# A feed forward in one unit of 1024 tokens, with Strassen's product in both projections

## The chip, the cores and the metric

The kernel runs on one NeuronCore of a Trainium2 chip. The metric is the device time of one execution in microseconds (us). Five engines take part: TensorE (PE, matmuls; PEld is its weight load), VectorE (DVE), ScalarE (ACT), GpSimd (POOL), and SyncE (SP), which here only issues DMA transfers.

## The reference

One layer of a streaming encoder for a prompt of 1024 tokens and 128 sample tokens (8 sequences of 16). The change is in its last step, the feed forward:

```python
D_MODEL = 1024
D_FF = -(-8 * D_MODEL // (3 * 256)) * 256        # 2816

def swiglu(x, w_in, w_out):
    g, u = jnp.split(x @ w_in, 2, axis=-1)
    return (jax.nn.silu(g) * u) @ w_out

def post_blocks(x, mix, mk, mv, w_mem_q, w_mem_o, w_ffn_in, w_ffn_out, ln_g, ln_b):
    x = layer_norm(ALPHA * x + mix, ln_g[0], ln_b[0])
    x = layer_norm(ALPHA * x + mem_attention(x, mk, mv, w_mem_q, w_mem_o), ln_g[1], ln_b[1])
    x = layer_norm(ALPHA * x + swiglu(x, w_ffn_in, w_ffn_out), ln_g[2], ln_b[2])
    return x
```

All data are float32. What comes ahead (the combined input projection, a gated linear recurrence, sliding window attention, the output projection, attention into 256 memory tokens) computes the same before and after.

## The kernel before, in words

*Precision.* A float32 operand is split into a part that a fast matmul keeps (`hi`, type fp32r; a ScalarE cast, L132) and a rest (`lo`, a VectorE subtraction, L133). A product is three matmuls: hi by hi, lo by hi, hi by lo (`mm3`, L93).

*Tokens.* Nine tiles of 128 rows; the third is the sample's. They go through the layer in three groups of three tiles. `mem_kv` projects the memory tokens and stores them from `kv_sb` to DRAM; then phase 2 starts, whose first matmuls belong to `out_proj` (weights `w_out`). The last step ahead of the feed forward is `mem_out` of group 2. The rows after the second norm are in DRAM (`x2_dram`; the profile names it x_scratch).

*Feed forward.* Two units: tiles 0 to 3 (512 tokens) and tiles 4 to 8 (640). `unit_operands` transposes a unit's rows (L97) and makes the seven right operands B11, T1, T2, B22, T3, B21, T4 of Winograd's form of Strassen's product, each in hi and lo; POOL makes the differences (L933). Tokens are halved, so a product has 256 or 320 columns. `hidden` computes two tiles of the hidden features, 11 pairs for a unit: four weight tiles of 128x1024 (512 KB) are loaded from `in_w_f`, their sums are made on POOL (L970, L975) and DVE (L974, L979), each of seven products has 24 matmuls, and ACT and DVE add the products up and apply the gate (`th`, L995 to L1001). The hidden features stay on the chip. `ffn` goes over parts of the features: some pairs of `hidden`, then `proj_rows`, the second projection, as a plain product with 512 columns that is added to the rows by DVE (L705). The second unit's operands are made while the first unit's last part runs.

*Order.* The code is a set of generators with ranks (`Order`): the one of the lowest rank whose operands should be ready goes on, on a clock that counts the cost of matmuls alone. A scheduler behind it then sets each engine's own order. Loads, and stores too, all go through SP's one queue, in order; one that waits holds up those behind it. Weights are loaded into three buffers (`w_raw`).

Of the kernel before, what the change touches and what calls it, by code (L numbers as in the profile page):

```python
# [18 lines left out]
P = 128  # L19
# [16 lines left out]
# tokens go in the order of ORDER: two tiles of the prompt, the samples (tile 8), the other tiles of the prompt  # L36
# [6 lines left out]
class Event:  # L43
    """a point on TensorE's clock from which a result is expected to be there"""
# [34 lines left out]
class TensorE:  # L79
    """TensorE with the products' cost added to the clock of an Order"""  # L80
# [19 lines left out]
def trunk(ctx, tc, I, O):  # L100
# [10 lines left out]
    wp = pool("wp")  # L111
# [6 lines left out]
    def bank(name):  # L118
        return pp[name][0].tile([P, 512], F32, name=name, bufs=pp[name][1])
# [41 lines left out]
    class Quads(list):  # L161
        """feature-major blocks [P, GW] in two parts, four to a slot"""
# [40 lines left out]
    def fm(wsrc, x, which="a", n=GW, w=None):  # L203
        """one block of columns, feature major"""
# [9 lines left out]
    ident = const.tile([P, P], F32, name="ident")  # L214
    make_identity(nc, ident)
    tri = const.tile([P, 640], U8, name="tri")
    own = const.tile([P, 8], F32, name="own")
    sinks = const.tile([P, 8], F32, name="sinks")
    sinks_s = const.tile([P, 2], F32, name="sinks_s")
    gnorm = const.tile([P, P], F32, name="gnorm")  # L220
# [3 lines left out]
    carry = const.tile([P, HGH, P], F32, name="carry")  # L224
    V.memset(carry, 0.0)
    starts = [const.tile([P, GW], F32, name=f"starts{i}") for i in range(2)]
# [142 lines left out]
    def hgrn(g, h, xt, tm):  # L369
# [53 lines left out]
        def body():  # L423
# [14 lines left out]
            # from chunks to pairs of chunks  # L438
# [45 lines left out]
    def hgrn_sample(h, qg, kdt, v, at, pl, po, sv):  # L484
        """the sample's tile: a chunk and a state for each of its sequences"""
# [25 lines left out]
    def finish(sb, mx, sk, nk):  # L511
        """rows of sb [P, n, .]: exp(s - max), normalised with the sink's share"""
# [12 lines left out]
    def swa_tile(p1, ip, t, pos, q, ak, av):  # L525
        """heads 2 ip and 2 ip + 1 of both groups, one tile of queries over its own and the preceding tile of keys"""
# [105 lines left out]
    def proj_rows(src, wsrc, evac, which, ahead=(), nt=GT, by_tile=False):  # L632
        """rows of nt tiles; src: blocks [P, nt * P] in two parts"""
# [205 lines left out]
    def mem_sample(p2, qf, ot, ready):  # L839
# [5 lines left out]
        def cache():  # L845
            """the next part of the caches, four sequences to a tile"""
# [55 lines left out]
    class Unit:  # L902
        def __init__(self, t0, nt, pieces, tmp, row, th):
            self.t0, self.nt, self.n = t0, nt, nt * 64
            self.pieces, self.tmp, self.row, self.th = pieces, tmp, row, th
            self.ready = Event()

        def operand(self, op, kt):
            for k0, hi, lo in self.pieces[op]:
                if k0 <= kt < k0 + hi.shape[1]:  # L910
                    return hi[:, kt - k0], lo[:, kt - k0]

    def unit_operands(u):
        """a unit's rows, transposed, to the products' operands in two parts"""
        rows = [u.row() for _ in range(u.nt)]
        for t in range(u.nt):
            for q, r in enumerate(rows[t]):
                nc.sync.dma_start(out=r, in_=x2_dram[u.t0 + t][:, q * 512:(q + 1) * 512])
        yield 4000.0
        for t in range(u.nt):  # L920
            b = {}
            for q in range(2):
                ps = transposes(rows[t][q])
                st = u.tmp("stage")
                S.copy(st[:, :512], ps)
                v = st[:, :512].rearrange("p (k e c) -> p k e c", k=4, e=2)
                for e in range(2):
                    b[f"B{q + 1}{e + 1}"] = v[:, :, e]
            tt = [u.tmp("tt")[:, :512].rearrange("p (a k c) -> p a k c", a=2, k=4) for _ in range(2)]
            for n in range(4):  # L930
                b[f"T{n + 1}"] = tt[n // 2][:, n % 2]
            for o, x, y in (("T1", "B12", "B11"), ("T3", "B22", "B12"), ("T2", "B22", "T1"), ("T4", "B21", "T2")):
                G.tensor_tensor(b[o], b[x], b[y], op=ALU.subtract)  # L933
            c = slice(t * 64, t * 64 + 64)
            for o in OPS:
                for k0, hi, lo in u.pieces[o]:
                    src = b[o][:, k0:k0 + hi.shape[1]]
                    S.copy(hi[:, :, c], src)
                    (G if o == "T4" else V).tensor_tensor(lo[:, :, c], src, hi[:, :, c].bitcast(F32), op=ALU.subtract)  # L939
# [320 lines left out]
```

## Time and profile before

| | us |
|---|---|
| median of 3 runs | 1669.98 (1669.64 to 1675.53) |
| profiled execution | 1669.8 (its span) |
| PE busy | 1618.8 (97%) |
| DVE busy | 1235.5 (74%) |
| ACT busy | 735.8 (44%) |
| POOL busy | 244.2 (15%) |
| feed forward's first matmul | 858.45 |

The profile is of one execution, and its span is the whole of that execution's time as far as it is recorded. A row of a group gives line, engine, operation, output and inputs, shape and count, then busy us, mean ns of one, the idle time ahead and what ended it. Matmul records overlap: each one's own length (280 to 390 ns) is longer than the distance between two starts, and it is the distance that counts.

### The profile page before, as it was taken

The page shows a single profiled execution, that of the slowest core. Times are in us where ns is not written, and L with a number is a line of the kernel's source. Part 1 is how long each engine was busy: PE and PEld are TensorE (multiplying, and loading weights), DVE is VectorE, ACT ScalarE, POOL GpSimd, SP SyncE. Part 2 cuts the span into 40 slices and gives each one's busy share as a digit, 9 for nine tenths or more (in the row PEclk, how much of TensorE's full clock was granted, in tenths as well). Part 3 has the DMA queues.
Part 4 walks back from the last instruction along what each step waited for, and adds up shares of the span by engine and source line. Part 5 has one row for each costly group of instructions (what it writes and reads, how often), then busy time and mean ns, then how long its engine had stood idle before and what let it go on. Part 6 is the DMA issues. An engine that isn't in the chain of part 4 may idle for free. (4 is left out here: it accounts for less than half of the span.)

```text
span 1669.8 us, 26720 instructions
## 1 busy us (share of the span) xinstructions
PE 1618.8 (97%) x10341; PEld 1477.3 (88%) x10341; DVE 1235.5 (74%) x2161; ACT 735.8 (44%) x1471; POOL 244.2 (15%) x234
## 2 busy tenths in 40 slices
PE   8999999999999999999988999999989999999998
PEld 7998999999878987879878898989888999989896
DVE  6887688788568666787799577667898757566568
ACT  4543455445543555224645244345543424334241
POOL 1111121111000000000232110212232111111111
PEclk9999999999999999999999999999999999999999
DMA  7453343333884588646332523132543313131231
GB/s 244 128 179 125 93 151 102 105 115 108 277 313 149 169 274 311 234 138 227 101 114 91 176 89 127 64 101 91 175 168 122 101 58 107 51 101 64 89 100 65
DMA packets 84800, 233.65 MB, mean 140 GB/s; under 512 B 10048, under 2 KB 28352, under 8 KB 84672
## 3 DMA queue, kind: packets, MB, share of 16 engines
q1 hardware_dynamic: 84672, 231.93, 42.4%
q8 instruction: 81, 1.33, 0.3%
q14 instruction: 47, 0.39, 0.1%
HBM read 210.86 MB, written 20.97 MB: 139 GB/s over the span
## 5 line engine op out<-in xcount | busy, mean ns | idle before, releaser
L133 DVE TENSOR_TENSOR w_lo<-w_raw,w_hi 128x1024 fp32r<-128x1024 f32 (+1 forms) x279 | 343.1, 1232 | 166.4 <-ACT w_hi L132 165.5
L132 ACT CAST w_hi<-w_raw 128x1024 fp32r<-128x1024 f32 (+1 forms) x279 | 290.0, 1041 | 323.8 <-PE a L93 147.0
L93 PE MATMUL a<-w_hi,h 128*128 128x512 f32 x756 | 242.6, 394 | 5.2 <-DVE rows L705 2.6
L93 PE MATMUL a<-w_hi,q_hi 128*128 128x256 f32 (+1 forms) x576 | 197.0, 344 | 3.5 <-ACT w_hi L132 2.9
L93 PE MATMUL a<-w_lo,q_hi 128*128 128x256 f32 (+1 forms) x576 | 197.0, 342 | 1.9 <-DVE w_lo L133 1.8
L93 PE MATMUL a<-w_hi,q_lo 128*128 128x256 f32 (+1 forms) x576 | 195.4, 339 | 0.0
L93 PE MATMUL a<-q_hi,w_hi 128*128 128x384 f32 x528 | 186.8, 354 | 6.8 <-ACT q_hi L132 4.3
L93 PE MATMUL a<-q_hi,w_lo 128*128 128x384 f32 x528 | 180.1, 341 | 0.0
L93 PE MATMUL a<-q_lo,w_hi 128*128 128x384 f32 x528 | 179.9, 341 | 0.0
L93 PEld LDWEIGHTS a<-w_hi,h 128*128 128x128 f32 x756 | 141.8, 188 | 38.5 <-ACT h L1000 3.6
L132 ACT CAST w_hi<-w_s 128x1024 fp32r<-128x1024 f32 x88 | 92.2, 1048 | 181.3 <-PE a L93 87.9
L133 DVE TENSOR_TENSOR w_lo<-w_s,w_hi 128x1024 fp32r<-128x1024 f32 x88 | 134.6, 1533 | 35.9 <-ACT w_hi L132 35.9
L93 PE MATMUL a<-w_lo,h 128*128 128x512 f32 x378 | 148.2, 392 | 0.0
L970 POOL TENSOR_TENSOR w_s<-w_raw 128x1024 f32<-128x1024 f32 x22 | 54.8, 2492 | 490.6 <-DMA w_raw<-in_w_f_dram 428.7
L93 PE MATMUL a<-x,w_hi 128*128 128x256 f32 x704 | 126.3, 280 | 0.0
L93 PEld LDWEIGHTS a<-w_hi,q_hi 128*128 128x128 f32 x576 | 108.5, 188 | 17.9 <-ACT w_hi L132 3.3
L705 DVE SCALAR_TENSOR_TENSOR rows<-rows,a 128x512 f32<-128x512 f32 x123 | 82.7, 682 | 55.6 <-PE a L93 55.4
L93 PEld LDWEIGHTS a<-w_lo,q_hi 128*128 128x128 f32 x576 | 108.6, 189 | 16.8 <-DVE w_lo L133 3.4
L93 PEld LDWEIGHTS a<-w_hi,q_lo 128*128 128x128 f32 x576 | 108.6, 188 | 12.7 <-issue 0.5
L93 PEld LDWEIGHTS a<-q_hi,w_hi 128*128 128x128 f32 x528 | 100.6, 191 | 11.7 <-ACT q_hi L132 4.4
L93 PEld LDWEIGHTS a<-x,w_hi 128*128 128x128 f32 x704 | 108.1, 188 | 0.3
L93 PEld LDWEIGHTS a<-q_lo,w_hi 128*128 128x128 f32 x528 | 100.8, 191 | 1.9 <-issue 0.9
(247 smaller groups left out, 3662.5 us busy)
## 6 DMA issues: line engine op xcount, KB each, us to landing
w_raw<-in_w_f_dram SPq DMA_DIRECT2D x110, 512.0 KB, 3.6
w_raw<-in_w_fm_dram SPq DMA_DIRECT2D x41, 512.0 KB, 4.1
w_raw<-in_w_tm_dram SPq DMA_DIRECT2D x24, 512.0 KB, 3.6
w_raw<-in_w_out_dram SPq DMA_DIRECT2D x24, 512.0 KB, 5.4
w_raw<-in_w_mq_dram SPq DMA_DIRECT2D x24, 512.0 KB, 4.4
w_raw<-in_w_mo_dram SPq DMA_DIRECT2D x24, 512.0 KB, 4.1
w_s<-in_w_f_dram SPq DMA_DIRECT2D x22, 512.0 KB, 4.4
ln_gb<-in_ln_dram SPq DMA_DIRECT2D x16, 512.0 KB, 6.7
```

The costliest lines, as they stand in the source:

```text
L93: return self.eng.matmul(out, lhsT, rhs, **kw)
L132: S.copy(hi, src)
L133: V.tensor_tensor(lo, src, hi.bitcast(F32), op=ALU.subtract)
L705: V.scalar_tensor_tensor(y[t][:, hs], y[t][:, hs], scale, ps, op0=ALU.mult, op1=ALU.add)
L970: G.tensor_tensor(s1, a21, a22, op=ALU.add)
```

## The change

The prompt's eight tiles become one unit: 1024 tokens, 512 columns a product. `all_operands` makes its operands after `mem_out` of group 2. The first projection runs for all 11 pairs (`hidden`), with all sums of weights on POOL, and ends with the hidden features' own Strassen operands, of which seven a pair are stored to DRAM (`h_scratch`, L1051). The second projection then follows as a second stage: weights from two tiles a pair with sums on POOL (`prepare`), the operands of the features loaded again (`hq`, L1132), five parts of the pairs, two sets of blocks of 256 tokens. The sample's tile no longer belongs to a unit: its hidden features come by plain float32 matmuls of 128 columns (`sample_hidden`, run by `filler` at rank 10), in part beside `all_operands`, the rest during the second projection; they too go through DRAM (`hs_scratch`). Pools are closed and opened between the stages, the buffers of one stage lying where those of another were. The last norm puts half of its scaling on ACT and POOL (`final_norm`). The diff's core:

```diff
-UNITS = ((0, 4, ((0, 6), (6, 12), (12, 16), (16, 22))),
-         (4, 5, ((0, 2), (2, 6), (6, 10), (10, 14), (14, 18), (18, 22))))
+TILES = (0, 1, 3, 4, 5, 6, 7, 8)
+SAMPLE = 2
+PAIRS = FT // 2
+PARTS = ((0, 3), (3, 5), (5, 7), (7, 9), (9, 11))
...
+    def sample_hidden(i):
+        ps = bank("b")
+        for e in range(2):
+            w = []
+            for q in range(2):
+                w.append(ff["sample_w"]())
+                nc.sync.dma_start(out=w[q], in_=I["w_f1"][i, e * 2 + q])
+            for z in range(2):
+                for kt in range(KT):
+                    T.matmul(ps[:, cols(e * 2 + z)], w[kt // 4][:, cols(z * 4 + kt % 4)], xs[:, kt],
+                             start=kt == 0, stop=kt == KT - 1)
...
+        nc.sync.dma_start(out=hs_dram[:, i], in_=h)
...
     def hidden(f1, ops, i):
...
+            t = f1.tile([P, 1024], F32, name=name, tag="w", bufs=8)
...
+        G.tensor_tensor(s1, a21, a22, op=ALU.add)
+        G.tensor_tensor(s2, s1, a11, op=ALU.subtract)
+        G.tensor_tensor(a21, a11, a21, op=ALU.subtract)
+        G.tensor_tensor(s4, a12, s2, op=ALU.subtract)
...
+        gated(th[1], [(a, X[0], X[1]), (b, m1[0], m1[1])])
+        G.tensor_tensor(t2, th[1][:, b], t1, op=ALU.subtract)
+        G.tensor_tensor(th[0][:, b], th[1][:, b], th[0][:, b], op=ALU.subtract)
+        G.tensor_tensor(t4, th[1][:, a], t2, op=ALU.subtract)
+        for o, src in (("T2", t2), ("B22", th[1][:, b]), ("T3", th[0][:, b]), ("B21", th[1][:, a]), ("T4", t4)):
+            store(o, src)
...
+        def f2w(name):
+            return f2.tile([P, 1024], F32, name=name, tag="w", bufs=5)
+
+        def prepare(i):
+            w0, w1, s12, s34 = (f2w(x) for x in ("w0", "w1", "s12", "s34"))
+            for n, t in enumerate((w0, w1)):
+                nc.sync.dma_start(out=t, in_=I["w_f2"][n, i])
...
+            G.tensor_tensor(s1, a21, a22, op=ALU.add)
+            G.tensor_tensor(s2, s1, a11, op=ALU.subtract)
+            G.tensor_tensor(s4, a12, s2, op=ALU.subtract)
+            G.tensor_tensor(s3, a11, a21, op=ALU.subtract)
...
+                S.copy(hi, src)
+                (G if name in ("A21", "A22") else V).tensor_tensor(lo, src, hi.bitcast(F32), op=ALU.subtract)
...
+            nc.sync.dma_start(out=q, in_=h_dram[bs[0] // 2, OPS.index(o), :, i0:i1, c:c + n])
+            S.copy(hi, q)
+            (G if o in ("T1", "T3", "T4") else V).tensor_tensor(lo, q, hi.bitcast(F32), op=ALU.subtract)
...
+        for i in range(PARTS[0][1]):
+            prepare(i)
+        for b in range(4):
+            for e in range(2):
+                y[b, e] = f2.tile([P, 1024], F32, name="y", bufs=8)
+                out_rows(x2_dram, b, e, y[b, e], None)
...
+            yield from blocks(part, (0, 1), last)
+            yield from filled(part[1])
+            yield from sample(part, n == 0, last)
...
+            yield from blocks(part, (2, 3), last)
+            for _ in range(*part):
+                if len(prepared) < PAIRS:
+                    prepare(len(prepared))
```

How the instructions stand at the places that the prediction speaks of. First SP's queue where phase 2 begins, before (kv_sb is what `mem_kv` stores):

```order
L143 DMA w_raw<-in_w_out_dram 128x1024
L199 DMA raw<-mix_scratch 128x384 x2
L264 DMA out_dram<-kv_sb 128x512
L266 DMA mem_kv_scratch<-kv_sb 128x256 x2
L264 DMA out_dram<-kv_sb 128x512
L266 DMA mem_kv_scratch<-kv_sb 128x256 x2
L143 DMA w_raw<-in_w_out_dram 128x1024
L714 DMA rows<-in_xtok_dram 128x1024 x3
L143 DMA w_raw<-in_w_out_dram 128x1024
L264 DMA out_dram<-kv_sb 128x512
```

And the same place after:

```order
L719 DMA rows<-in_xtok_dram 128x1024 x3
L689 DMA ln_gb<-in_ln_dram 128x1024 x2
L269 DMA out_dram<-kv_sb 128x512
L271 DMA mem_kv_scratch<-kv_sb 128x256 x2
L269 DMA out_dram<-kv_sb 128x512
L271 DMA mem_kv_scratch<-kv_sb 128x256 x2
L148 DMA w_raw<-in_w_out_dram 128x1024 x3
L204 DMA raw<-mix_scratch 128x384 x2
```

The first three loads of w_out stood ahead of the last stores of kv_sb; now they stand behind them.

TensorE after the last `mem_out`, before (x, B and T are a unit's operands):

```order
L93 MATMUL a<-w_lo,q_hi 128x512
L93 MATMUL a<-w_hi,q_lo 128x512
L93 MATMUL a<-x_9109,w_hi 128x256
L93 MATMUL a<-x_9110,w_hi 128x256
L93 MATMUL a<-x_9109,w_lo 128x256
```

And after (xs is the sample's transposed rows, x_row a tile's rows):

```order
L95 MATMUL a<-w_lo,q_hi 128x512
L95 MATMUL a<-w_hi,q_lo 128x512
L95 MATMUL b<-xs,w_raw 128x128 x20
L99 MATMUL b<-ident,x_row 128x128 x8
L95 MATMUL b<-xs,w_raw 128x128 x16
L99 MATMUL b<-ident,x_row 128x128 x8
L95 MATMUL b<-xs,w_raw 128x128 x16
```

A unit's products followed directly; now the operands' transposes and the sample's matmuls stand between.

SP's queue where the first projection gives way to the second: before, in the last unit (L946 loads `hidden`'s weights, L143 `proj_rows`'s):

```order
L946 DMA w_s<-in_w_f_dram 128x1024
L946 DMA w_raw<-in_w_f_dram 128x1024 x3
L946 DMA w_s<-in_w_f_dram 128x1024
L143 DMA w_raw<-in_w_f_dram 128x1024 x4
L946 DMA w_raw<-in_w_f_dram 128x1024 x3
```

And after, from the last pair's stores on (w_12906 to w_12991 are the weights of the first three `prepare`):

```order
L1051 DMA h_scratch<-th 128x2x256 x3
L1051 DMA h_scratch<-t_12845 128x2x256
L1111 DMA w_12906<-in_w_f_dram 128x1024
L1111 DMA w_12907<-in_w_f_dram 128x1024
L1075 DMA y<-x_scratch 64x1024 x3
L1111 DMA w_12948<-in_w_f_dram 128x1024
L1111 DMA w_12949<-in_w_f_dram 128x1024
L1075 DMA y<-x_scratch 64x1024 x3
L1111 DMA w_12990<-in_w_f_dram 128x1024
L1111 DMA w_12991<-in_w_f_dram 128x1024
L1075 DMA y<-x_scratch 64x1024 x10
L962 DMA w_s<-in_w_f_dram 128x1024 x2
```

Weight loads of the two projections followed one another; now the second projection's loads stand behind the last store of h, and the rows y, the sample's weights w_s and then hq behind those.

POOL at that place, before:

```order
L970 TENSOR_TENSOR w_s<-w_raw 128x1024
L975 TENSOR_TENSOR w_raw<-w_raw 128x1024
L692 TENSOR_TENSOR rs<-rs,mhalf 128x1 x5
```

And after (t_12845 is the last pair's T4; s are sums of weights, A22l and A21l the rests of weights):

```order
L1065 TENSOR_TENSOR t_12845<-th,t_12844 128x512
L1114 TENSOR_TENSOR s_12908<-w_12907 128x512
L1117 TENSOR_TENSOR s_12909<-w_12906,w_12907 128x512
L1115 TENSOR_TENSOR s_12908<-s_12908,w_12906 128x512
L1123 TENSOR_TENSOR A22l<-w_12907,A22h 128x512
L1116 TENSOR_TENSOR s_12909<-w_12906,s_12908 128x512
L1123 TENSOR_TENSOR A21l<-w_12907,A21h 128x512
L1114 TENSOR_TENSOR s_12950<-w_12949 128x512
```

POOL had two sums a pair and nothing for the second projection; now it has six operations for each pair's second-projection weights.

More of the change, by code (lines that the diff above doesn't have):

```diff
@@ L110, in trunk @@
     sm = pool("sm")
-    wp = pool("wp")
+    left = ctx.enter_context(ExitStack())
+    wp = left.enter_context(tc.tile_pool(name="wp", bufs=1))
+    first = ctx.enter_context(ExitStack())
+    cp = first.enter_context(tc.tile_pool(name="cp", bufs=1))
     right = ctx.enter_context(ExitStack())
@@ L223, in trunk @@
     V.memset(mhalf, -0.5)
-    carry = const.tile([P, HGH, P], F32, name="carry")
+    carry = cp.tile([P, HGH, P], F32, name="carry")
     V.memset(carry, 0.0)
-    starts = [const.tile([P, GW], F32, name=f"starts{i}") for i in range(2)]
+    starts = [cp.tile([P, GW], F32, name=f"starts{i}") for i in range(2)]
     for t in starts:
@@ L900, in trunk @@
     OPS = ("B11", "T1", "T2", "B22", "T3", "B21", "T4")
[L902 to L921, printed above, removed]
-            for q in range(2):
[L923 to L939, printed above, removed]
-            yield (6500.0 if u.t0 == 0 else 3500.0)
-        order.set(u.ready, 4000.0)
@@ L952, in hidden, with product @@
         X, Z, W = [], [], []
-        m0, m1 = ([u.tmp("m") for _ in range(2)] for _ in range(2))
-        def product(bk, which, w_src, op, start):
-            hi, lo = (wp.tile([P, 1024], F32R, name=x, bufs=N_W) for x in ("w_hi", "w_lo"))
-            split(w_src, hi, lo)
+        def product(bk, which, w, op, start):
+            pair = parts_of(w, *(f1.tile([P, 1024], F32R, name=x, bufs=3) for x in ("w_hi", "w_lo")))
             for z in range(2):
@@ new lines, in hidden, with out_rows @@
+        gated(th[1], [(a, X[0], X[1]), (b, m1[0], m1[1])])
[4 more added lines that the diff above has]
+            store(o, src)
+    def out_rows(dst, b, e, row, store):
+        for n in range(2):
+            at = dst[TILES[2 * b + n]][e * 64:e * 64 + 64]
+            r = row[n * 64:n * 64 + 64]
+            if store is None:
+                nc.sync.dma_start(out=r, in_=at)
+            else:
+                nc.sync.dma_start(out=at[:, store], in_=r[:, store])
```

350 lines of the change are left out of this document (245 added, 105 removed).

## The prediction

> **What bounds the kernel now.** I read the page's busy shares first, then the chain that ended last, the waits of TensorE, the groups, the DMA issues and a few stretches of the timeline.
>
> ```profile
> PE 1618.8 (97%) x10341; PEld 1477.3 (88%) x10341; DVE 1235.5 (74%) x2161; ACT 735.8 (44%) x1471; POOL 244.2 (15%) x234
> ```
>
> TensorE is the bound; nothing else is near it. So the time is the price of its matmuls plus the holes between them. The chain's pieces (start, length, what) price the matmuls:
>
> ```profile
> 1022.63 38.35 PE a L93 x192
> 1060.98 2.85 PE b L93 x24
> 1415.68 17.52 PE a L93 x84
> 1433.20 3.52 PE b L93 x24
> 1630.01 31.64 PE a L93 x144
> 1661.67 0.69 DVE rows L705
> ```
>
> 24 matmuls of 256 columns take 2.85 us (118.7 ns each), 24 of 320 take 3.52 (146.7 ns). The piece of 192 holds 48 of 256 columns and 144 of 512: (38.35 - 5.70) / 144 = 226.7 ns. The piece of 84 holds 24 of 320 and 60 of 512: (17.52 - 3.52) / 60 = 233.3 ns. I take the middle, 230 ns, for 512 columns; both ends go into the range. TensorE ends at 1630.01 + 31.64 = 1661.65, then 8.2 us of norm and stores remain.
>
> By the Trainium skill (TensorE: Matmul & The Clock Gate, Part 1) the distance is N / 2.4 GHz + 2.5 ns, 215.7 ns at 512, which would give 109.2 and 135.8 ns at 256 and 320. The rows differ (118.7, 146.7, 226.7 to 233.3) and decide; by the page the matmul term below would be about -4.6 instead of -17.6 us.
>
> The timeline shows where the feed forward starts, what a plain f32 matmul of 128 columns costs, and the boundary after the memory keys and values:
>
> ```profile
> 858.45 0.40 PE L93 MATMUL a<-x,w_hi 128*128 128x256 f32 x2
> ...
> 88.39 0.39 PE L93 MATMUL b<-carry,hg_a 128*128 128x128 f32 x2
> 88.61 0.39 PE L93 MATMUL b<-hg_b 128*128 128x128 f32 x2
> ...
> 461.89 0.49 PE L93 MATMUL a<-w_hi,q_hi 128*128 128x512 f32 x1 [0.68 <-ACT kv_sb L263]
> ```
>
> The f32 matmul has two records in 0.22 us. The feed forward is 1661.65 - 858.45 = 803.2 us long. Its waits (total, times, longest), and those of the stretch ahead of it:
>
> ```profile
> PE b L93 <- DVE w_lo L133: 16.4, 11, 4.2
> PE a L93 <- DVE rows L705: 2.6, 2, 1.5
> PE a L93 <- ACT h L1000: 2.6, 2, 1.8
> ...
> PE a L93 <- ACT w_hi L132: 2.9, 1, 2.9
> PE a L93 <- DVE w_lo L133: 2.0, 2, 1.4
> ```
>
> A long gap costs twice. The 4.2 us wait stands in these windows (the last three numbers are the granted clock, the DMA engines' busy share and GB/s):
>
> ```profile
> 1226.00:1230.00 4.00, 3.62 (x25) 3.35 (x23) 3.59 (x7) 2.77 (x7) 3.12 (x4) 1.00 0.99 293
> 1230.00:1234.00 4.00, 0.26 (x2) 0.00 (x0) 4.00 (x3) 1.70 (x3) 2.35 (x1) 0.76 0.54 218
> 1234.00:1238.00 4.00, 3.54 (x13) 3.54 (x14) 4.00 (x7) 0.43 (x1) 0.00 (x0) 0.50 0.39 131
> 1238.00:1242.00 4.00, 4.00 (x26) 4.00 (x25) 4.00 (x7) 1.87 (x3) 0.00 (x0) 0.88 0.46 153
> ```
>
> After it the clock was 0.50 for 4 us and 0.88 for the next 4: 2.0 + 0.5 = 2.5 us lost beside the gap. The same section of the Trainium skill says half rate after an idle window of about 3.4 us, until a busy window has passed; the trace agrees, and by the page each long hole would add about 1.7 us.
>
> **The change part by part.** Prices of the other engines:
>
> ```profile
> L970 POOL TENSOR_TENSOR w_s<-w_raw 128x1024 f32<-128x1024 f32 x22 | 54.8, 2492 | 490.6 <-DMA w_raw<-in_w_f_dram 428.7
> L133 DVE TENSOR_TENSOR w_lo<-w_raw,w_hi 128x1024 fp32r<-128x1024 f32 x275 | 341.4, 1244 | 163.6 <-ACT w_hi L132 162.7
> L133 DVE TENSOR_TENSOR w_lo<-w_s,w_hi 128x1024 fp32r<-128x1024 f32 x88 | 134.6, 1533 | 35.9 <-ACT w_hi L132 35.9
> L132 ACT CAST w_hi<-w_raw 128x1024 fp32r<-128x1024 f32 x275 | 288.3, 1050 | 321.0 <-PE a L93 147.0 <-issue 44.7 <-PE b L93 42.0
> L933 POOL TENSOR_TENSOR tt<-stage,tt 128x256 f32<-128x256 f32 x18 | 15.2, 846 | 0.7
> L995 ACT ACTIVATE th<-m 128x512 f32<-128x512 f32 x22 | 13.9, 632 | 34.1 <-DVE m L987 33.9
> L996 DVE SCALAR_TENSOR_TENSOR th<-th,m 128x512 f32<-128x512 f32 x22 | 18.6, 846 | 4.2 <-ACT th L995 4.2
> L97 PE MATMUL b<-ident,rows 128*128 128x128 f32 x144 | 19.9, 273 | 0.9 <-issue 0.6 <-DMA rows<-x_scratch 0.4
> ...
> w_raw<-in_w_f_dram SPq DMA_DIRECT2D x110, 512.0 KB, 3.6
> w_raw<-in_w_out_dram SPq DMA_DIRECT2D x24, 512.0 KB, 5.4
> w_s<-in_w_f_dram SPq DMA_DIRECT2D x22, 512.0 KB, 4.4
> x_scratch<-rows SPq DMA_DIRECT2D x18, 256.0 KB, 2.0
> ```
>
> *Matmuls.* Removed: 1848 of 256 and 1848 of 320 columns, 1848 x 0.1187 + 1848 x 0.1467 = 490.5 us. Added for it: 1848 of 512 and the sample's 352 f32 ones, 425.0 + 352 x 0.222 = 425.0 + 78.1 = 503.1. Second projection: 1188 of 512 go (273.2), 924 + 132 come (242.9). Sum: +12.6 - 30.3 = **-17.6**. Row transposes are 72 in both.
>
> *Holes removed.* 803.2 - 490.5 - 273.2 - 40 transposes at 19.9 / 144 = 0.138 (5.5) leaves 34.0 us of waits and slow clock in the old feed forward: **-34**. Of the 4.9 us ahead of it I take **-4**, as DVE and ScalarE no longer prepare a unit there.
>
> *Phase boundary.* SP issues in its order, and its timeline shows these rows:
>
> ```profile
> 448.95 0.33 SPq L143 DMA_DIRECT2D w_raw<-in_w_out_dram  x1
> ...
> 461.16 0.34 SPq L264 DMA_DIRECT2D out_dram<-kv_sb  x1
> ...
> 464.19 1.26 SPq L684 DMA_DIRECT2D ln_gb<-in_ln_dram  x2
> ```
>
> Before, three w_out loads stand ahead of the last kv_sb stores, which wait for ScalarE. After, all stand behind: issue at 464.2, landing 3.6 to 5.4 later, cast 1.05, so the first matmul moves from 461.9 to 468.9 to 470.6: **+8**. Queued behind the same stores are raw<-mix_scratch, also needed there.
>
> *Operand stage.* TensorE has 64 transposes (8.8 us) and 192 f32 matmuls (42.6). Each half pair needs two loads of 512 KB, from three buffers. The buffer that the second matmul group wants comes free at the 12th of 16 matmuls before it (2.7 us), then a load of 3.6 to 4.4: the period is about 5.5 us instead of 3.55. Twelve of them are 66 us, of which transposes fill little in the first half: **+16** over the 51, range 2 (loads of 2.0, the nearest shorter DMA row) to 24. The operands' work on POOL (four differences, one rest, 8 tiles at some 4.5 us = 36) and ScalarE hides in it.
>
> *Start of the first projection.* a11's load stands on SP behind the last store of the sample's features, which waits for tanh and two DVE steps (about 1.6 us); then load 4.0 and cast 1.05, w_lo beside the first matmuls: **+8** with the issue and semaphores, range 4 to 9.
>
> *First projection.* A pair is 168 x 0.230 = 38.6 us. POOL has 4 x 2.49 + 4 x 1.4 = 15.6, ScalarE about 12 (seven casts at 1.05, the rest copies and tanh at 0.63 per 512), DVE about 19 (seven w_lo at 1.24, six sums and four products of 512 to 1024 at 0.85 per 512). All hide; if POOL were not free, s1 would be late by one 2.5 us operation. Taken **+2**.
>
> *Between the projections.* The 128x512 price on POOL is not in the trace: by the rows 0.85 (256) and 2.49 (1024) it is 1.4, bounds 1.25 (half of 1024) and 1.7 (twice 256). From the end Te of the last matmul: tanh 0.63, two DVE steps 0.85 each, T4's difference 1.4, so T4's store leaves SP at Te + 3.7. Only behind it stand the first second-projection weights (w_12906, w_12907), landing at +7.9. POOL then has six operations a set; w_12949 waits for the buffer of w_12906, free after five (+14.9), lands at +18.9; w_12991 waits for the next five (+25.9). Behind it on SP are ten y loads of 256 KB, two w_s and the first hq: issue 14 x 0.33 = 4.6, and 4.6 MB at the 293 GB/s of the window whose DMA engines were full (0.99) is 15 us, so hq is there at +38, cast and rest done at +40. Sixteen f32 matmuls fit before it. Hole: **+38**, range 28 (short prices throughout) to 44.
>
> *Second projection.* A part of two pairs has about 50 us of TensorE. POOL has 12 prepares, taps and rests: some 32 us at 1.4; DVE and ScalarE less. But hq has two buffers and its loads queue behind weights that wait for POOL, and in the last part the hq loads stand behind stores of y. No row shows this; ends 0 and 40, taken **+10**, near the low end since TensorE's share is the largest. Tail: two POOL operations at 1.4 in place of two DVE steps at 0.7: **+1.4**.
>
> *Clock.* Three holes over 4 us at 2.5: **+7** (0.5 less for the overlap with waiting).
>
> Sum: 1669.8 - 17.6 - 34 - 4 + 8 + 16 + 8 + 2 + 38 + 10 + 1.4 + 7 = **1704.6**; I say 1703. The profiled execution's span, 1669.8, is the median of the runs (1669.98) within 0.2 us.
>
> **The rivals.**
>
> *Loads run ahead (faster).* Nearly every added hole is a load's latency. If 512 KB lands in 2.0 us, as the 256 KB stores do, then the boundary is +5, the operand stage +2, the start +5, the hole 3.7 + 2.3 + 7 + 2 + 7 + 2 + 2 less 3.6 = 23, the second projection +3, the clock +6: 1669.8 - 55.6 + 5 + 2 + 5 + 2 + 23 + 3 + 1.4 + 6 = 1662, and with 226.7 ns for 512 about 9 less, 1653. It decides at about 2.1 us a load. For it: 293 GB/s moves 512 KB in 1.8 us. Against: the median of 110 loads is 3.6.
>
> *Half the holes (about equal).* The hole and the boundary are as priced, but the sample's matmuls run at TensorE's pace (+2) and the second projection has none: 1703 - 14 - 10 = 1679, 1670 at the faster cadence. For it: the transposes could cover loads. Against: three buffers.
>
> *POOL bounds the second projection (slower).* POOL's operations beside DVE slow down: DVE's w_lo is 1.24 us alone and 1.53 beside POOL's sums. With 2 us an operation POOL's 32 us a part become 46, with waits between the engines over TensorE's 50: some 8 us a part, five parts, 1743. It decides at 2.2 us an operation. The Trainium skill (GPSIMD Engine Reference, 1. Specifications) states that POOL shares its memory interfaces with VectorE and contends where DVE has two inputs; w_lo's two rows agree.
>
> **How the numbers follow.** Forecast case 0.55 (1682 to 1725), loads ahead 0.17, half the holes 0.14, POOL 0.14. A measurement tells about 0.5% (8.3 us) from no change: faster is under 1661.6, slower over 1678.3. Loads ahead is faster in 0.14 and same in 0.03; half the holes is same in 0.09 and slower in 0.05; the others are slower. So 0.14, 0.12, 0.74. The range runs to 1658 and 1742, with about 0.1 left out on either side.
>
> **What would show it.** Right: a gap of 28 to 44 us on TensorE with POOL and DMA busy, about 40 us after the last `th`; waits of `b<-xs,w_raw` for DMA totalling over 10 us; 8 us at the boundary; matmuls of 512 at 227 to 233 ns in pairs of 38.6 us without gaps; TensorE's busy share down to some 93%. Wrong: a gap under 20 us, or the operand stage near 51 us; then I mis-sized loads. If the second projection exceeds 320 us, POOL is the bound there.

## The result and the profile after

The changed kernel takes 1761.28 us (median of 4 runs, 1756.98 to 1765.44) against 1671.24 us (median of 4) of the kernel before: ratio 1.0528, 95% interval 1.0504 to 1.0553. It is slower, as forecast, but by 90 us and not by 33, which is above the upper end of the forecast range, 1742. The profiled execution spans 1758.1 us. Its busy shares:

```profile
PE 1617.7 (92%) x9065; PEld 1392.5 (79%) x9065; DVE 1129.5 (64%) x2006; ACT 687.5 (39%) x1398; POOL 522.6 (30%) x418
```

TensorE is busy for as long as before (1617.7 and 1618.8 us) and idle for 89 us more (140.4 in place of 51.0). Where, the windows show (us, then busy us and instructions of PE, PEld, DVE, ACT and POOL, then granted clock, DMA share, GB/s): operand stage, first projection, hole, second projection.

```profile
854.60:928.50 73.90, 54.54 (x450) 50.51 (x448) 39.51 (x69) 31.39 (x79) 35.15 (x41) 0.98 0.61 211
928.50:1361.90 433.40, 433.26 (x1848) 346.72 (x1848) 232.47 (x209) 138.82 (x175) 185.67 (x86) 1.00 0.28 94
1361.90:1406.40 44.50, 0.02 (x1) 0.02 (x1) 20.54 (x19) 13.75 (x24) 28.72 (x21) 0.54 0.82 219
1406.40:1747.70 341.30, 298.08 (x1376) 242.28 (x1376) 204.86 (x280) 112.33 (x197) 186.21 (x137) 0.94 0.43 135
```

The first projection runs 433 us without a hole. The second takes 341.3 us for 1056 matmuls of 512 columns and the sample's last 160. In the rows below w_s are the sample's weights, tap is ScalarE's copy of a finished sum out of its PSUM bank (one buffer), and y are the rows to which a sum is added, by POOL from tap or by VectorE. TensorE's waits from the hole to the end (total, times, longest):

```profile
PE b L95 <- DMA w_s<-in_w_f_dram: 49.7, 3, 44.5
PE x L95 <- ACT tap L1142: 17.5, 4, 6.8
PE z L95 <- DVE y L1145: 8.0, 1, 8.0
```

The chain's pieces give the cadence of 512 columns in the two projections, and the timeline the boundary of the phases:

```profile
936.26 5.60 PE b L95 x24
...
1441.18 4.08 PE x L95 x18
```

```profile
469.11 1.22 PE L95 MATMUL a<-w_hi,q_hi 128*128 128x512 f32 x2 [9.47 <-ACT w_hi L137]
```

**The hole.** SP's timeline from the last store of h on:

```profile
1364.94 1.29 SPq L1111 DMA_DIRECT2D w<-in_w_f_dram  x2
...
1368.14 11.44 SPq L1111 DMA_DIRECT2D w<-in_w_f_dram  x2
...
1381.47 8.63 SPq L1111 DMA_DIRECT2D w<-in_w_f_dram  x2
1390.16 6.34 SPq L1075 DMA_DIRECT2D y<-x_scratch  x10
1397.24 1.44 SPq L962 DMA_DIRECT2D w_s<-in_w_f_dram  x2
```

And POOL's first sum of the first and of the third set (that of the second starts at 1382.70):

```profile
1372.17 1.26 POOL L1114 TENSOR_TENSOR s<-w 128x512 f32<-128x512 f32 x1 [7.71 <-DMA w<-in_w_f_dram]
...
1393.74 1.26 POOL L1114 TENSOR_TENSOR s<-w 128x512 f32<-128x512 f32 x1 [2.33 <-DMA w<-in_w_f_dram]
```

Two pairs of loads keep SP for 11.44 and 8.63 us, since their second one waits for a buffer that POOL frees; each round is 11 us, and then ten loads of y stand ahead of what TensorE waits for, the sample's weights w_s. The chain is the predicted one.

**The second projection.** PSUM is the memory that TensorE writes to. A sum in one of its banks must be copied or added out before TensorE can write its next product there. S1 to S4 are the sums of weights, S4h and S4l the cast and the rest of one, hq, hh and hl a loaded operand of the features, its cast and its rest. Two of TensorE's long waits, with ScalarE's rows that end them:

```profile
1504.28 1.70 POOL L1116 TENSOR_TENSOR s<-w,s 128x512 f32<-128x512 f32 x1
...
1506.01 0.62 ACT L1122 CAST S4h<-s 128x512 fp32r<-128x512 f32 x1 [2.20 <-POOL s L1116]
1506.54 0.58 ACT L1142 COPY tap<-x 128x512 f32<-128x512 f32 x1
...
1507.17 0.79 PE L95 MATMUL x<-S2h,hh 128*128 128x512 f32 x1 [6.65 <-ACT tap L1142]
...
1625.53 0.58 ACT L1142 COPY tap<-x 128x512 f32<-128x512 f32 x1 [4.44 <-POOL y L1143]
...
1626.17 0.80 PE L95 MATMUL x<-S2h,hh 128*128 128x512 f32 x1 [6.79 <-ACT tap L1142]
```

In both, TensorE's next product goes into bank x, which ScalarE must copy out first. In the first wait the sum in x was complete by 1498 and tap's buffer free since 1494.6, when POOL's last addition ended; but ScalarE works its queue off in order, and the copy stands behind the casts of S1, S3, S2 and S4 of the next weights, each of which waits for POOL's sum. In the second wait the copy does wait for tap's one buffer, that is for POOL's addition y, which stands in POOL's queue behind sums and rests of the next weights. The clock falls in such a gap; windows of 4 us around the first:

```profile
1504.00:1508.00 4.00, 0.83 (x2) 0.74 (x3) 2.20 (x3) 1.62 (x3) 4.00 (x4) 0.70 0.00 0
1508.00:1512.00 4.00, 2.85 (x7) 1.75 (x7) 3.23 (x4) 1.10 (x2) 3.31 (x3) 0.50 0.87 293
1512.00:1516.00 4.00, 4.00 (x11) 3.10 (x10) 1.27 (x2) 0.62 (x1) 3.59 (x4) 0.52 0.86 303
```

After 6.65 us of waiting TensorE runs at half clock until 1515.8, for more than 8 us. Over the three middle parts POOL was by no means full (110.54 of 173 us), but from 1489.7 to 1510.6, around the stall, it had no gap (20.87 of 20.90 us): its work for the next weights comes in bursts.

```profile
1460.00:1633.00 173.00, 150.41 (x666) 121.88 (x665) 112.21 (x129) 67.48 (x120) 110.54 (x77) 0.93 0.39 124
...
1489.70:1510.60 20.90, 13.74 (x70) 11.03 (x69) 16.86 (x16) 8.56 (x15) 20.87 (x13) 0.88 0.37 125
```

### The profile page after: what moved, and what is told of

It reads as the page before. It is cut to its first block, busy times and chain, and to the rows that moved or that the text cites. A ratio compares the mean times of both kernels' runs of the same rounds, so it can differ in the third digit from the quotient of the medians.

```text
span 1758.1 us, 24635 instructions
## 1 busy us (share of the span) xinstructions
PE 1617.7 (92%) x9065; PEld 1392.5 (79%) x9065; DVE 1129.5 (64%) x2006; ACT 687.5 (39%) x1398; POOL 522.6 (30%) x418
## 4 chain that ended last, share of the span: by engine, by line
PE 76%; DMA 7%; DVE 6%; POOL 5%; issue 2%; ACT 2%; SPq 1%; POOLq 0%; ACTq 0%; DVEq 0%
PE a L95 45%; PE b L95 21%; PE x L95 4%; PE b L99 2%; DMA w_raw<-in_w_f_dram 2%; PE z L95 2%; PE s L95 1%; PE w L95 1%; DMA w<-in_w_f_dram 1%; DMA w_s<-in_w_f_dram 1%; POOL y L1143 1%; POOL s L1116 1%; DMA w_raw<-in_w_mv_dram 1%; DVE y L1145 1%; DVE sc L548 1%
## 5 line engine op out<-in xcount | busy, mean ns | idle before, releaser
L138 DVE TENSOR_TENSOR w_lo<-w_raw,w_hi 128x1024 fp32r<-128x1024 f32 (+1 forms) x169 | 205.4, 1218 | 119.6 <-ACT w_hi L137 118.8
L137 ACT CAST w_hi<-w_raw 128x1024 fp32r<-128x1024 f32 (+1 forms) x169 | 174.8, 1036 | 197.6 <-PE a L95 82.6
L138 DVE TENSOR_TENSOR w_lo<-a,w_hi 128x1024 fp32r<-128x1024 f32 x44 | 73.2, 1664 | 81.8 <-ACT w_hi L137 80.8
L95 PE MATMUL a<-T_l,w_hi 128*128 128x512 f32 x264 | 104.1, 394 | 0.0
L95 PE MATMUL a<-T_h,w_hi 128*128 128x512 f32 x264 | 104.1, 394 | 0.0
L95 PE MATMUL a<-T_h,w_lo 128*128 128x512 f32 x264 | 104.1, 394 | 0.0
L95 PEld LDWEIGHTS a<-q_hi,w_lo 128*128 128x128 f32 x528 | 100.5, 190 | 1.4 <-DVE w_lo L138 1.1
L137 ACT CAST w_hi<-a 128x1024 fp32r<-128x1024 f32 x44 | 46.2, 1051 | 136.2 <-PE a L95 67.0
L138 DVE TENSOR_TENSOR w_lo<-s,w_hi 128x1024 fp32r<-128x1024 f32 x33 | 64.0, 1940 | 39.0 <-ACT w_hi L137 39.0
L95 PE MATMUL b<-xs,w_s 128*128 128x128 f32 x320 | 41.2, 288 | 51.1 <-DMA w_s<-in_w_f_dram 49.7
```

The lines of the kernel that those rows point to most:

```text
L95: return self.eng.matmul(out, lhsT, rhs, **kw)
L137: S.copy(hi, src)
L138: V.tensor_tensor(lo, src, hi.bitcast(F32), op=ALU.subtract)
```

## The experiments

e1 to e12 and e14 are one execution each. They are compared by the length of the stage that the edit touches, from its first to its last matmul; a row of the windows gives it. Whole times are less sharp: the sample's first matmul starts anywhere between 853.1 us (e2) and 859.4 (e5) where the code up to there is the same.

**Taps on VectorE (e1).**

```diff
-            if key in y and bn is None and e == half == 0:
+            if False:
```

> One edit: the 32 sums that went by a copy on ScalarE (tap, one buffer) and an addition on POOL (y<-y,tap, 1.41 us each, 45 us in all) are made by VectorE straight from PSUM, as the other sums are. In the changed kernel the second projection took 341.6 us (1406.4 to 1748), 282 of them matmuls at full clock. Theory A (POOL's order): TensorE waits for a PSUM bank whose tap waits for the one buffer, which waits for an addition that stands on POOL behind sums of weights. Then the waits for ACT tap (17.5 + 2.1 us) go, POOL has 45 us less, and the second projection takes 300 to 320 us. Theory B (renewal of the weights: loads, five buffers, three sets): the stalls come back under other names, 335 to 345 us. Theory C (features' operands loaded again, hq with two buffers): 335 to 345 us, with waits for hh and hl in their place.

The second projection took 326.9 us, 14.4 less; POOL's busy time in it fell by 44:

```profile
1410.10:1737.00 326.90, 292.42 (x1376) 240.38 (x1376) 212.36 (x311) 95.25 (x165) 142.30 (x105) 0.95 0.45 140
```

Less than theory A hoped for, more than B or C allow. The waits did not vanish; they are now VectorE's, and the longest, 6.6 us, is for the same product as the 6.65 us before: VectorE's addition stands behind the rests of S1 to S4, whose casts wait for POOL's sums.

```profile
PE x L95 <- DVE y L1145: 10.0, 3, 6.6
```

The time of the whole was 1749.18 us.

**Two tap buffers (e2).**

```diff
-                t = f2.tile([P, 512], F32, name="tap")
+                t = f2.tile([P, 512], F32, name="tap", bufs=2)
```

> One edit: the tap has two buffers in place of one, every engine's order is the same. Theory A in its narrow form (one buffer): the waits for ACT tap fall from 19.6 us to under 8 and the second projection from 341.6 to some 328 us. If POOL's order as a whole is the cause, a second buffer helps once and then fills: 336 to 341 us. B and C: no change, 341 us.

```profile
1405.60:1743.00 337.40, 297.42 (x1376) 241.66 (x1376) 206.77 (x279) 111.29 (x197) 186.50 (x137) 0.95 0.44 136
```

337.4 us, 4 less. The wait of 6.65 us is still there, since the copy stands behind the casts as before; the one of 6.79 us, which hung on the buffer, is down to 2.17. Whole: 1755.21 us.

```profile
1508.84 0.80 PE L95 MATMUL x<-S2h,hh 128*128 128x512 f32 x1 [6.66 <-ACT tap L1142]
```

**No renewal (e3).**

```diff
-            ws = [prepared[i] for i in range(*part)]
+            ws = [prepared[i % 3] for i in range(*part)]
...
             for _ in range(*part):
-                if len(prepared) < PAIRS:
-                    prepare(len(prepared))
+                pass
```

> Left out: the weights of the second projection's pairs 3 to 10 are neither loaded nor summed nor split; the first three pairs' are used again in their place. All matmuls, features' operands, taps and sums stay. Theory A and theory B: with the renewal gone POOL has some 70 us less and no load is waited for, so the second projection falls to 285 to 300 us. Theory C: hq's loads still pace it, 325 to 340 us. The hole ahead of it (44.7 us) stays in each.

```profile
1407.80:1712.80 305.00, 286.58 (x1376) 237.15 (x1376) 143.38 (x231) 78.46 (x133) 112.87 (x89) 0.97 0.42 124
```

305.0 us (whole: 1725.11): renewing the weights costs 36.3 of the 341.3 us. The features' operands, all still loaded again, do not pace it (theory C falls). What stays beside the matmuls is mostly the last part, where the norms run: 15.8 of the 18.4 us in which TensorE is idle, at a mean clock of 0.89. Its longest wait, 8.0 us for VectorE's y, is there as before; what makes it was not tried.

```profile
1635.10:1712.80 77.70, 61.91 (x288) 49.08 (x287) 52.22 (x98) 17.37 (x33) 41.48 (x37) 0.89 0.43 115
```

**A first part of one pair (e4).**

```diff
-PARTS = ((0, 3), (3, 5), (5, 7), (7, 9), (9, 11))
+PARTS = ((0, 1), (1, 3), (3, 5), (5, 7), (7, 9), (9, 11))
...
-            for _ in range(*part):
+            for _ in range(2):
```

> One edit: the first part of the second projection has one pair and not three (parts 1, 2, 2, 2, 2, 2), so one set of weights is prepared ahead of its first product. If the hole of 44.7 us is three rounds of load and POOL sums (11 us each, as the timeline shows w_12907, w_12949 and w_12991 landing at 1372, 1382.7 and 1393.7), two rounds go and the hole is 22 to 28 us, with the y loads now setting its end. If the y loads and the sample's weights on SP's queue set it alone, it is 40 to 45. The second projection itself has one part more (28 sums on VectorE and POOL more) and renews two sets in the time of one pair: 341.6 becomes 345 to 360, so the whole is 1745 to 1765 us.

```profile
1366.80:1396.10 29.30, 0.00 (x0) 0.00 (x0) 7.36 (x7) 4.65 (x8) 11.34 (x9) 0.58 1.01 267
1396.10:1745.20 349.10, 303.12 (x1376) 245.05 (x1376) 235.10 (x315) 125.63 (x234) 215.73 (x160) 0.93 0.44 136
```

The hole is 29.3 us, 15 less, though two rounds of 11 went: the DMA engines were full for all of it (1.01), so the loads, most of them of y, now set its end. The second projection took 8 us more, the whole 1760.70. Both effects are there, rounds and loads.

**No sums of the renewed weights (e5).**

```diff
...
+            if i < 3:
...
+            else:
+                s1, s2, s4, s3 = a21, a11, a12, a22
```

> Left out: POOL's four sums of weights a pair for pairs 3 to 10 of the second projection (32 operations of 1.3 to 1.6 us, 47 us in all); the raw quarters are split in their place, so the loads, casts and rests stay. Without any renewal the second projection fell from 341 to 305 us. Theory A (POOL's order): most of that comes from the sums, 305 to 320 us here. Theory B (loads, five buffers, the wait for a set to come free): 330 to 341 us.

```profile
1409.90:1726.20 316.30, 290.88 (x1376) 238.23 (x1376) 186.54 (x279) 111.65 (x197) 140.26 (x105) 0.96 0.46 146
```

316.3 us (whole: 1738.37): 25.0 of renewal's 36.3 us come with the 32 sums. Loads, casts and rests, which stayed, cost the other 11. The waits for tap fall from 19.6 us to the 2.3 of this row, so both of the long ones above are gone:

```profile
PE w L95 <- ACT tap L1145: 2.3, 3, 0.8
```

VectorE's operations, as many as before, also took 18 us less (186.5 in place of 204.9), as fewer of them ran beside POOL's sums. How much of the 25.0 us comes this way, and how much from the places in the queues, is not parted.

**More buffers for the sample's weights (e6).**

```diff
-        ff["sample_w"] = raw_tile
...
+            k = turn[0] % 11
+            if k < 3:
+                return raw_tile()
+            return wp.tile([P, 1024], F32, name="w_raw", tag="w_hi" if k < 7 else "w_lo", bufs=N_W)
...
+        ff["sample_w"] = any_tile
```

> One edit: the sample's weights in the operand stage rotate over 11 buffers (the three of w_raw and the eight of w_hi and w_lo, idle there) and not three. The stage took 65.6 us from the end of mem_out to the last matmul of the sample, against 51 us of TensorE work. Theory L (each load waits for one of three buffers): 51 to 56 us, and the waits for DMA w_raw (10.5 us) go. Rival (the operands' work on POOL, ScalarE and VectorE paces it): 62 to 66 us, with waits for T_l and B_l.

```profile
856.30:915.70 59.40, 50.32 (x450) 49.91 (x448) 37.90 (x68) 31.12 (x79) 35.03 (x41) 0.98 0.71 249
```

From 73.9 to 59.4 us, start of the first projection included (whole: 1749.07). The chain's last piece of the sample's matmuls (898.03, 10.73 long) ends 52.5 us after the stage's start, in theory L's 51 to 56; the wait for a11 stays:

```profile
898.03 10.73 PE b L95 x96
...
910.54 3.99 DMA a<-in_w_f_dram
```

**The rows y later (e7).**

```diff
                 for b, hs in zip(bs, operand(*part, bs, h)):
+                    if (b, e) not in y:
+                        y[b, e] = f2.tile([P, 1024], F32, name="y", bufs=8)
+                        out_rows(x2_dram, b, e, y[b, e], None)
...
-        for b in range(4):
-            for e in range(2):
-                y[b, e] = f2.tile([P, 1024], F32, name="y", bufs=8)
-                out_rows(x2_dram, b, e, y[b, e], None)
```

> One edit: the rows y are loaded with the first operands and no longer ahead of them, so ten loads of 256 KB go from in front of hq and w_s. Theory R (rounds of load and POOL sums, 11 us each): the first product's first two matmul groups can start after about 14 us, but the third pair's weights still come at 1393.7 + 1.5; TensorE starts earlier on the sample (hole 15 to 25) and waits again, together 33 to 38 us of holes in place of 44.7 + 3.7. Rival (the 4.6 MB ahead of hq set it): all holes together 20 to 28 us.

```profile
1364.70:1375.10 10.40, 0.03 (x1) 0.00 (x0) 1.98 (x3) 2.27 (x4) 3.83 (x4) 0.74 0.96 329
1375.10:1738.10 363.00, 307.22 (x1376) 248.22 (x1376) 218.63 (x295) 123.54 (x217) 212.30 (x155) 0.91 0.48 144
```

The first hole is 10.4 us and smaller ones follow; hole and second projection together take 373.4 us in place of 385.8, 12.4 less (whole: 1750.33). Theory R is nearer: taking the y loads away does not bring the third set of weights sooner; its first sum starts 32.5 us behind the hole's start, and 31.8 in the changed kernel.

**The weights' pool kept (e8).**

```diff
-    left.close()
...
-    wp = left.enter_context(tc.tile_pool(name="wp", bufs=1, reuse_waits="tile"))
```

> One edit: the weights' pool is not closed and opened again between the phases (xs goes to the other side of the memory, its transposes to the start of the feed forward), by which SP's order at the boundary is that of the kernel before: three loads of w_out ahead of the last kv_sb stores. If the order alone made the 9.5 us hole there, it falls to under 1.5 us and the end of mem_out comes 8 to 9 us earlier. If the stretch behind it was bound by something else anyway, the end of mem_out moves by 0 to 4 us. The rest stays as it is, save about 1 us more for the sample's transposes, which nothing covers there now.

The first matmul of w_out starts at 460.42, with a wait of 0.80 in place of 9.47. The order on SP made that hole. The sample's first matmul, now behind 1.3 us of its own transposes, starts 9.8 us earlier, at 844.8; by the spread given above this is right to a few us. The whole: 1755.59.

```profile
460.42 0.50 PE L95 MATMUL a<-w_hi,q_hi 128*128 128x512 f32 x1 [0.80 <-ACT kv_sb L268]
```

**All of it, and POOL relieved (e9).** The edits of e1, e6, e7 and e8, and:

```diff
-            G.tensor_tensor(s4, a12, s2, op=ALU.subtract)
-            G.tensor_tensor(s3, a11, a21, op=ALU.subtract)
...
+                    V.tensor_tensor(a12, a12, s2, op=ALU.subtract)
+                    V.tensor_tensor(a11, a11, a21, op=ALU.subtract)
...
-        G.tensor_tensor(y[:, h0], y[:, h0], gb[0][:, h0], op=ALU.mult)
+        V.tensor_tensor(y[:, h0], y[:, h0], gb[0][:, h0], op=ALU.mult)
```

> The edits of e1 (taps on VectorE), e6 (more buffers), e7 (y later) and e8 (weights' pool kept) together, and for POOL's share: s4 and s3 are made by VectorE in place of a12 and a11 (two of four sums of weights leave POOL, six buffers of which a set now takes three), and the last norm's scaling goes from POOL to VectorE. Theory A (POOL's order paces the second projection): stalls in the parts nearly vanish, as without renewal, so the second projection falls from 341 to 295 to 305 us and the hole to some 25 in all; with 12.8 at the operand stage and 8 at the boundary the whole is 1680 to 1700 us. Rival (VectorE, with 32 sums, 16 sums of weights and the norm more, becomes what TensorE waits for): second projection 315 to 330 us, waits for DVE y and DVE hl, the whole 1705 to 1725 us.

1707.11 us, 54 less than the changed kernel and 36 more than the kernel before. Hole and second projection take 350.5 us in place of 385.8:

```profile
1342.60:1693.10 350.50, 295.89 (x1377) 241.71 (x1376) 247.99 (x362) 107.64 (x188) 121.80 (x87) 0.93 0.52 158
```

POOL has 122 us left of 215 in hole and second projection (28.7 + 186.2), VectorE 248 of 350, and behind the start, whose four waits for w_s and hh make 26 us (10.5 and 11.7 the longest), the longest waits are VectorE's: the rival's account.

```profile
PE x L95 <- DVE rs L1080: 8.0, 1, 8.0
PE x L95 <- DVE y L1145: 6.2, 4, 5.4
```

**The same with a first part of one pair (e10).**

> e9 with the first part of one pair (e4's edit). By the rounds of loads the hole falls by some 10 us more against e9, and the part more costs VectorE 28 sums of 0.68 us (19 us) beside the matmuls: if POOL was the pace and VectorE has room, 1675 to 1695 us, 5 to 10 less than e9; if VectorE is now the pace, 5 to 15 more than e9.

```profile
1335.30:1695.50 360.20, 301.85 (x1377) 245.98 (x1376) 258.55 (x397) 110.27 (x202) 121.99 (x93) 0.92 0.52 154
```

1709.81 us; hole and second projection take 360.2 us, 10 more than in e9. With VectorE as the pace a part more costs more than a round less saves.

**Preparing spread (e11).**

```diff
+            if n > 0 and len(prepared) < PAIRS:
+                prepare(len(prepared))
             yield from blocks(part, (2, 3), last)
-            for _ in range(*part):
+            for _ in range(2 if n == 0 else 1):
```

> One edit: after the first two parts, one of the two sets of weights of a part is prepared in its middle (behind the blocks 0 and 1) and one at its end, not two at its end; a third set is free for it. POOL's operations are the same in number and length (some 186 us in the second projection). If POOL's order at the ends of parts makes the stalls (its sums stand in a row ahead of the additions that free the tap), the waits for ACT tap halve and the second projection falls from 341 to 325 to 332 us. If POOL's amount makes them, it stays at 336 to 345 us.

```profile
1409.60:1748.90 339.30, 297.43 (x1376) 241.00 (x1376) 207.39 (x279) 111.50 (x197) 187.89 (x137) 0.94 0.44 135
```

339.3 us and 1761.15 in all: no change. But the edit hardly reached POOL's queue, whose order the scheduler sets: POOL's first 22 operations of the stage come in the same order as without it, and the later ones move by a few places. At the first stall the copy stands behind the cast of S4 again:

```profile
1511.25 0.62 ACT L1122 CAST S4h<-s 128x512 fp32r<-128x512 f32 x1 [1.76 <-POOL s L1116]
...
1512.41 0.79 PE L95 MATMUL x<-S2h,hh 128*128 128x512 f32 x1 [7.44 <-ACT tap L1142]
```

So this run does not decide between order and amount; what sums that are spread on POOL itself would give was not tried.

**e9 with the same edit (e12).**

> e9 with e11's edit. With POOL already relieved there is less to spread: if the remaining 37 us of gaps in e9's second projection are renewal at the ends of parts, 5 to 12 us less than e9's 1707 us; if they are VectorE's (which e9 loads with sums, taps and the norm), 0 to 4 us less.

```profile
1333.70:1683.20 349.50, 297.14 (x1377) 242.93 (x1376) 245.43 (x362) 107.60 (x188) 124.02 (x87) 0.93 0.53 159
```

1697.54 us, but hole and second projection take 349.5 us against e9's 350.5; here too POOL's sums, counted from the end of the first projection, start within 4 us of where they did. Of the 9.6 us between the two times all but 1 lie ahead of the second projection, 8.5 of them ahead of the feed forward, where nothing differs (the sample's transposes start at 842.0 in place of 850.5). This is the shortest time of the changed kernel, and it does not beat the kernel before.

**The kernel before with all sums on POOL (e13).**

```diff
-        V.tensor_tensor(s2, s1, a11, op=ALU.subtract)
+        G.tensor_tensor(s2, s1, a11, op=ALU.subtract)
...
-        V.tensor_tensor(s1, a12, s2, op=ALU.subtract)
+        G.tensor_tensor(s1, a12, s2, op=ALU.subtract)
```

> The kernel before with one part of the change alone: all four sums of weights of the first projection on POOL (two of them, 1.22 and 1.39 us, were VectorE's; 44 in all, 57 us). In the changed kernel the first projection ran 432 us with no wait of TensorE at all, with this split. Theory (VectorE's load makes the 18.7 us of waits for w_lo in the old feed forward): 5 to 15 us faster, ratio 0.991 to 0.997. Rival (those waits come at the ends of parts, where norms and operands load VectorE and POOL alike, and POOL at 2.5 us a sum is later than VectorE was): same within 3 us, or 5 to 20 us slower, with waits for w_s of POOL.

1697.81 us (median of 5 runs, the kernel before 1671.88), ratio 1.0135 (95% interval 1.0112 to 1.0158): 1.35% slower, some 23 us, the rival's side and a little past its 20. ScalarE's casts there wait for the second sum that moved (total, times, longest) 48.1 us, where the kernel before has the 9.2 us of the second row for the same sum on VectorE, and TensorE for ScalarE's copies behind them:

```profile
ACT w_hi L132 <- POOL w_s L979: 48.1, 11, 6.8
...
ACT w_hi L132 <- DVE w_s L979: 9.2, 11, 2.6
```

```profile
PE a L93 <- ACT m L968: 18.9, 13, 4.0
```

So it is not the split of the sums that made the changed kernel's first projection free of holes. There a tile's loads are issued about a pair ahead, into eight buffers, and a pair has 39 us; that this is the reason was not tried by itself.

**Sums on VectorE (e14).**

```diff
-            G.tensor_tensor(s1, a21, a22, op=ALU.add)
...
+            E = G if i < 3 else V
+            E.tensor_tensor(s1, a21, a22, op=ALU.add)
...
```

> One edit: the four sums of weights of pairs 3 to 10 of the second projection are made by VectorE (32 operations, 0.7 to 1.4 us) and not by POOL (32 of 1.3 to 1.6 us, 47 us). The link from load to sum to cast to rest stays; POOL's amount falls as in e5, which left the sums out and took 316 us for the second projection against 341. If POOL's amount is what counts: 315 to 325 us. If the link itself (a sum between load and cast, in order with other work) is what counts: 333 to 345 us, with waits for DVE y in place of ACT tap.

```profile
1409.70:1741.00 331.30, 296.82 (x1376) 241.31 (x1376) 221.79 (x312) 111.83 (x197) 143.68 (x105) 0.95 0.45 139
```

331.3 us, 10 less (whole: 1753.16), between the two theories: POOL's occupancy, net of what VectorE now carries, is 10 of the 25 us. The other 15 are the sum as a link between load and cast, or VectorE's own load; the runs do not part these. The waits for ACT tap fall from 19.6 to 3.8 us, those for DVE y rise from 9.5 to 15.9.

## Why the prediction was wrong, step by step

The sum gave 1704.6 us for an execution that took 1758.1. By its steps, against the trace:

- *Matmuls.* 512 columns cost 233.3 ns in the first projection (5.60 us for 24) and 226.7 in the second (4.08 for 18), the two ends and not the middle. First projection with its 2 us of waits: 433.4 in place of 427, +6.4.
- *Phase boundary:* right; first matmul at 469.1 (468.9 to 470.6 forecast), and e8 shows that SP's order makes it. Ahead of the feed forward 4.5 us more were saved than I took, which is within the 6 us by which executions differ there.
- *Operand stage and start:* right; 73.9 in place of 75.4, and by the named mechanism (e6).
- *Hole:* right in mechanism, 44.5 in place of 38, just past the range's 44. e4 and e7 show both of its halves, rounds and y loads.
- *Second projection:* this is the step that failed, "taken +10, near the low end since TensorE's share is the largest". The stage took 341.3 us against 288.4 (242.9 + 35.5 + 10), +52.9, nearly the whole miss. Its matmuls at 226.7 ns and the sample's 160 at 0.222 are 274.9 us; 66.4 are stalls and slow clock, beyond my upper end of 40. POOL's work for a part was priced about right, 36.8 us (110.54 over three) in place of 32. Wrong was that it hides beside TensorE's 50: it comes in bursts, and TensorE's banks are not emptied until the burst has passed. The wait that I named was wrong too: for casts of the loaded features (hh) TensorE waited 4.2 us, for ScalarE's tap 19.6 and for VectorE's y 9.5. e3 puts 36.3 of the 66.4 us on the renewal of the weights, e5 25.0 of these on their sums, and e1 14.4 on the taps, which share POOL with the sums, so the three don't add. The other 30.1 us stay in e3, most of them in the last part, and their cause is open.
- *Clock.* I counted three holes at 2.5 us. The second projection adds gaps of its own, after which the granted clock is 0.50 (above); its mean there was 0.94. My 7 us stand apart in the sum while the trace holds them within its stages, which gives 7 back: -4.5 - 1.5 + 6.4 + 6.5 + 52.9 + 0.8 (tail, 10.4) - 7 = 53.6.

The POOL rival named the place and, at 1743 us, was nearest, but for its reason it asked for more: "It decides at 2.2 us an operation". Sums took 1.26 to 1.75 us and POOL was 64% busy over the middle parts. By my own sign ("If the second projection exceeds 320 us, POOL is the bound there") POOL is the bound, and its mean share does not show it. It doesn't need to be full on average: ScalarE's copy was ready to run and stood behind four casts that wait for POOL's sums, or it waited for an addition that stands behind other operations on POOL, and VectorE's additions stand behind rests in the same way when they are moved there (e1). VectorE takes POOL's place as soon as it gets more work (e1, e9, e14). That the sums are what the queues wait for is shown by e5, where the waits for tap go with them; that the one buffer of tap is only part of it, by e2. Whether a copy placed ahead of the casts would end the stalls was not tried. I had weighed the engines' busy shares where I ought to have followed one product's chain through three queues, as I had done for the hole, where it came out.

Against the kernel before, the feed forward takes 893.1 us (854.6 to 1747.7) in place of 803.2. By their cadences its matmuls cost some 15 us less, an estimate (748.7 in place of 763.7), but TensorE's busy time there is no shorter, 785.9 us in place of the 778.5 of this row, as the records of matmuls at half clock are longer (0.63 us in place of 0.39):

```profile
858.45:1661.65 803.20, 778.54 (x4925) 721.49 (x4923) 586.61 (x702) 331.13 (x505) 138.50 (x78) 0.99 0.31 102
```

And three things that the old form hid stand open: operands made with nothing to run beside them but a stage paced by loads, a hole where one projection must end before the other starts, and weights of the second projection that now need sums in the time that matmuls alone left.

## What to carry to other kernels

Fewer matmuls help only while what prepares their operands is covered: price every product as load, sum, cast, rest, matmul, copy out and addition through the in-order queues, and not by each engine's share. A mean share hides bursts: POOL was 64% busy over three parts and without a gap for the 20.9 us around the stall. Splitting one interleaved stage into two sequential ones buys a long stretch without waits and pays with a start-up hole as long as the rounds of its first buffers. Moving work to an idle engine pays only if nobody soon waits for it: the same sums on POOL cost TensorE no wait in the changed kernel's first projection and 1.35% (some 23 us) in the kernel before. That the earlier loads make this difference is likely and not shown.

## What the runs showed of the hardware

Rests of 128x512 on VectorE took 0.68 us while POOL was idle and up to 1.81 beside POOL's operations, and POOL's sums 1.26 us alone and 1.70 beside VectorE: both slow down, VectorE by far more than the kernel before let me expect (1.24 and 1.53 us at 128x1024). Two rows of VectorE in the hole, the first with POOL idle and the second beside a sum:

```profile
1370.92 0.68 DVE L1123 TENSOR_TENSOR A12l<-w,A12h 128x512 fp32r<-128x512 f32 x1
...
1378.03 1.75 DVE L1123 TENSOR_TENSOR S3l<-s,S3h 128x512 fp32r<-128x512 f32 x1
```

The same shape of matmul has two steady cadences, 233.3 and 226.7 ns, in the two projections of one execution; why was not tried.
